# Low parts of the early weights made by VectorE alone, and a new table of priorities, in a one-core transformer block

## The chip, the cores and the metric

The kernel runs on one core of one Trainium2 chip. A core has TensorE (PE in the rows: matmuls and transposes), VectorE (DVE), ScalarE (ACT), GpSimd (POOL) and SyncE (SP, which here only issues DMAs). Each engine takes its own instructions strictly in order and waits on semaphores for the others. The metric is device microseconds (us) of one execution, the median of several runs; lower is better.

## The reference

One transformer block on 512 tokens of width 1024, all in 32-bit floats. Of the reference, this is what is computed:

```python
u = rmsnorm(h, norm_mix_g) @ w_in
c_q, c_kv, k_rope, q_nsa, kv_cmp, kv_slc, kv_win, gate_logits = split(u)
o_mla = mla_mixer(c_q, c_kv, k_rope, ...)     # 8 heads over latent q and kv
o_nsa = nsa_mixer(q_nsa, kv_cmp, kv_slc, kv_win, gate_logits, ...)
#   = g0 * attention over 31 compressed blocks + g1 * over selected keys + g2 * over a window
mixed = concat(rmsnorm(o_mla), rmsnorm(o_nsa))
h = h + mixed @ w_out
f = rmsnorm(h, norm_ffn_g)
h = h + (silu(f @ w_gate) * (f @ w_up)) @ w_down
return rmsnorm(h, final_norm_g)
```

With 512 tokens every block is selected and the window covers every earlier token, so the kernel computes both sparse branches as causal attention with a bias.

## The kernel before, in words

Every factor of a matmul is kept as a high part (the value rounded to the type `fp32r`) and a low part (value minus high part), and a product is three matmuls: high by high, high by low, low by high (lines 168 to 170, `mm3`). So each weight is loaded as it is (`w_raw`, 128 partitions by 1024 values, 512 KB), then copied to the high part by ScalarE or VectorE (line 392, `w_hi`), and the low part `w_lo` is the difference of the two, made by VectorE (line 394) or GpSimd (line 395). Each weight is split in two pieces of 128x512. Both inputs and the output of a low part lie in SBUF.

The stages follow each other with overlap. (1) The tokens are normed and transposed (`xTh`, `xTl`), and the latent columns of `w_in` (`wl_raw`, split in eight pieces of 128x440) are multiplied for each of four token tiles, normed (`cn`) and turned. (2) Eight projections of 24 matmuls of 128x512 each: four of queries (`qs`), two of keys (`kh`, `kl`), two that feed the compression (`rr`); two compression products over weights of 512 KB twice (`in_nsa_cmp_w...`), and the values. (3) Sparse and latent softmax attention: scores (`sc`), minimum on VectorE (line 829), exponential on ScalarE (834), scaling on GpSimd (840), transposes (845), high part on ScalarE (850), low part on VectorE (853), value products (879). The latent weights `ukr` and `uqr` and the output weights `w_out` are split in the same way while this goes on. (4) The output product, and a feed-forward part that makes its own weight pieces elsewhere (line 1396). The change doesn't touch that code.

The rings: `w_raw` has two buffers in stages 1 and 2, the split pairs have three, and a product accumulates in one of two PSUM banks named `mm`. A bank comes free when VectorE has read it for the low part of its result (`qs`, line 371).

What sets the order: a planner in the kernel (`Plan`, lines 52 to 116) knows every job with an estimate of its time and lays the instructions of all engines out when the program is built. Where a job may run on either of two engines, it compares when each could start, plus an offset for that engine (`pdve`, `ppool`, `pact`). Between jobs that could start, the lower priority number goes first. All these numbers stand in the table `PRI` (line 123). The chip then runs the order as it was laid out. The DMA queues in the traffic around stage 2: SyncE issues the loads of `w_raw`, then the bias tables `bn` (8 DMAs) and `ga` (8 DMAs), in its own order; ScalarE issues the first halves of 24 background sums `T` of `w_down` and GpSimd the second halves (lines 1356 and 1357). The DMAs of the two hardware queues share eight completion counters (DMAHW0 to DMAHW7) in turn, and a DMA waits until the one before it on its counter has landed.

Of the kernel before, what the change touches and what calls it, by code (L numbers as in the profile page):

```python
# [13 lines left out]
OP = mybir.AluOpType  # L14
# [19 lines left out]
def f(ap):  # L34
    return ap.bitcast(F32)
# [19 lines left out]
class Plan:  # L55
# [11 lines left out]
    def add(self, ways, fn=None, after=(), pri=0.0, takes=(), frees=(), lag=None):  # L67

        if fn is not None:
            ways = [(ways[0], ways[1] * (1.07 if ways[0] == "pe" and ways[1] < 1374 else 1.0), fn)]  # L70
        j = Job(ways, [a for a in after if a is not None], pri, takes, frees, lag)
        self.jobs.append(j)
        return j
# [13 lines left out]
    def run(self):  # L87
        busy = {}
        clock, ready, waiting = {"dma": 3500.0, "dma2": 3000.0}, [], list(self.jobs)
        while waiting or ready:  # L90
# [4 lines left out]
            for j in ready:  # L95
                if any(len(self.slots[s]) < j.takes.count(s) for s in j.takes):
                    continue
                for way in j.ways:
                    e = way[0]
                    issue = 1150 if e in ("dma", "dma2") else 0  # L100
                    t = max([clock.get(e, 0.0)] + [a.seen(e) + issue for a in j.after] + [min(self.slots[s]) + issue for s in j.takes])
                    best.setdefault(e, []).append((t + (PRI.get("p" + str(e), 0) if len(j.ways) > 1 else 0), j.pri, j, way, t))
            assert best, "no job can go on"
            picks = []
            for e, c in best.items():
                t0 = min(x[0] for x in c)
                picks.append(min((x for x in c if x[0] <= t0 + PRI["slack"]), key=lambda x: x[1]))
            _, _, j, way, t = min(picks, key=lambda x: (x[0], x[1]))
# [11 lines left out]

PRI = dict(k0=-5.4, q0=-12.1, v=51.3, ck=-13.0, k1=8.0, cv=-9.5, q1=-9.4, q2=-38.5, q3=12.6, mla=38.1, out=180.9, slack=0, pdve=20.1,
           ppool=72.3, pact=310.9, wload=-10.3, wsplit=-28.4, mkeys=-2.4, lat=-20.5, cmp=-18.4, cuse=94.3, use=17.0, sout=77.2, seven=183.9,
           xoff=-26.6, xstep=-35.5, bias=-61.8, sums=912.1, bout=-82.5, loff=-25.8, woff=-217.5, wstep=301.5)


@with_exitstack
def block_kernel(ctx: ExitStack, tc: tile.TileContext, I, out):
    nc = tc.nc  # L130
    ve, se, pe, gp, sy = nc.vector, nc.scalar, nc.tensor, nc.gpsimd, nc.sync
# [140 lines left out]
    add = plan.add  # L272
    late = {}

    def t_act(n, sb=False):
        return (95 if sb else 55) + 0.833 * n
# [4 lines left out]
    def t_dve(n):  # L281
        return 70 + 1.042 * n

    def t_copy(n):
        return 70 + 0.521 * n
# [4 lines left out]
    def t_pool(n):  # L290
        return 90 + 2.22 * n
# [9 lines left out]
    def load(dst, src, pri, after=()):  # L301
        n = int(np.prod(dst.shape)) * 4
        return add(("dma", max(n / 360.0, 480)), lambda: sy.dma_start(dst, src), after, pri, lag=950)
# [86 lines left out]
    def split_pieces(h, l, raw, n, after, pri, takes=(), frees=()):  # L390

        j = add([("act", t_act(n, True), lambda: se.copy(h(), raw())), ("dve", t_copy(n), lambda: ve.tensor_copy(h(), raw()))],  # L392
                None, after, pri, takes=takes)
        return add([("dve", t_dve(n), lambda: ve.tensor_tensor(l(), raw(), f(h()), op=OP.subtract)),
                    ("pool", t_pool(n), lambda: gp.tensor_tensor(l(), raw(), f(h()), op=OP.subtract))], None, [j], pri, frees=frees)  # L395

    def weight(pl, srcs, shape, pri, raw, part, nraw, npart, after=(), pieces=2, parts=None):

        w = {}
        n = int(np.prod(shape))  # L400

        def start():
            w["raw"] = pl().tile([P] + list(shape), F32, name="w_raw", tag="w_raw", bufs=nraw)
            for dst, src in srcs:
                sy.dma_start(dst(w["raw"]), src)

        def piece(c):
            return slice(c * shape[0] // pieces, (c + 1) * shape[0] // pieces)

        def room():  # L410
            w["h"], w["l"] = parts() if parts else [pl().tile([P] + list(shape), F32R, name=nm, tag=nm, bufs=npart) for nm in ("w_hi", "w_lo")]

        j = w["load"] = add(("dma", n * P * 4 / 360.0), start, after, pri + PRI["wload"], takes=[raw], lag=950)
        j = w["room"] = add((None, 0), room, [j], pri + PRI["wsplit"], takes=[part])
        return w, [split_pieces(lambda c=c: w["h"][:, piece(c)], lambda c=c: w["l"][:, piece(c)], lambda c=c: w["raw"][:, piece(c)], n // pieces,
                                [j], pri + PRI["wsplit"] + 0.1 * c, frees=[raw] if c == pieces - 1 else ()) for c in range(pieces)]

# [13 lines left out]
    def load_wl(u):  # L431
        sy.dma_start(wl_raw[:, u, :, 0:416], win[:, 2 * u:2 * u + 2, 0:416])
        sy.dma_start(wl_raw[:, u, :, 416:440], win[:, 2 * u:2 * u + 2, C_GATE:C_END])

    wl_ready = []
    for u in range(4):
        j = add(("dma", 1300), lambda u=u: load_wl(u), pri=-97 + (u if u < 3 else 4), lag=950)
        wl_ready += [split_pieces(lambda u=u, k=k: wl_parts[u][0][:, k], lambda u=u, k=k: wl_parts[u][1][:, k], lambda u=u, k=k: wl_raw[:, u, k],
                                  440, [j], -95 + PRI["woff"] + PRI["wstep"] * u) for k in range(2)]
    x_loaded = [x0] + [[load(xt[t], xv[:, t, :], (-94, -92, -91)[t - 1])] * 2 for t in range(1, NT)]  # L440
# [88 lines left out]
    def bias_rows(c0, c1):  # L529
# [20 lines left out]
        return add(("act", 80), out, [j] + wl_ready, PRI["bout"], frees=["s"], lag=6000)  # L550

    table = split_pieces(lambda: txp[:, 0], lambda: txp[:, 1], lambda: tx, H, [g_row], PRI["bias"])
    choice_used = []
    bias0 = [bias_rows(0, 320), bias_rows(320, 640)]
# [527 lines left out]
    for t in range(NT):  # L1082
# [3 lines left out]
        def go(d=d, ts=ts):  # L1086
            d["o"] = bank("mm")
            mm3(d["o"], kvTh[:, ts], kvTl[:, ts], flat(late["uvh"]), flat(late["uvl"]), True, True)

        j = add(("pe", 640), go, uv_ready + lat_done, mpri + t, takes=["mm"])  # L1090
        vm_ready += split_values(lambda t=t: late["vm"][:, t], lambda d=d: d["o"].rearrange("p (h d) -> p h d", h=H), S, [j], mpri + t)
    for q in range(2):
        qc = slice(384 * q, 384 * q + 384)
        for t in range(NT):
            pri = mpri + 4 + 4 * q + t
# [16 lines left out]
            j = add(("pe", 480), lambda go=go: go(0), [uq_ready[q][0]] + lat_done, pri, takes=["mm"])  # L1112
            j = add(("pe", 480), lambda go=go: go(1), [j, uq_ready[q][1]], pri)
            j = add(("act", t_act(256)), lambda qd=qd, ov=ov: se.copy(qd()[:, :, 0:64], ov()[:, :, 0:64]), [j], pri)
            j = add(("dve", 480), rope, [j], pri, frees=["mm"])
# [192 lines left out]
    for nh in range(2):  # L1308
        for t in range(NT):
# [7 lines left out]
            j = None  # L1317
            for k in range(4):
                j = add(("pe", 640), lambda k=k, go=go: go(k), [j, wo[2 * nh + k // 2][1][k % 2]] + sparse_jobs, opri + 4 * nh + t, takes=["mm"] if k == 0 else (),
                        frees=["part2"] if t == NT - 1 and k % 2 else ())  # L1320
# [4 lines left out]
    for nh in range(2):  # L1325
        for t in range(NT):
# [7 lines left out]
            j = None  # L1334
            for k in range(4):
                j = add(("pe", 640), lambda k=k, go=go: go(k), [j, wo[4 + 2 * nh + k // 2][1][k % 2]] + latent_jobs, 300 + 4 * nh + t,
                        takes=["mm"] if k == 0 else (), frees=["part2"] if t == NT - 1 and k % 2 else ())
# [603 lines left out]
```

## Time and profile before

| | |
|---|---|
| median of 3 runs | 644.17 us (644.1 to 644.45) |
| the profiled execution, its own time | 642.98 us |
| its span in the trace | 641.1 us |
| TensorE busy | 609.1 us, 95% |
| VectorE busy | 520.9 us, 81% |
| ScalarE busy | 369.6 us, 58% |
| GpSimd busy | 177.0 us, 28% |

Shares of the whole span are means over stages with different limits. In the feed-forward part TensorE has no gap; in the 300 us before it, gaps and a busy VectorE alternate.

### The profile page before, as it was taken

How to read it: one execution, taken by the hardware profiler on the slowest of the kernel's cores; microseconds unless marked ns; L12 is line 12 of the kernel's file. 1: busy time of each engine (PE TensorE's matmuls, PEld its weight loads, DVE VectorE, ACT ScalarE, POOL GpSimd, SP SyncE). 2: the span in 40 equal slices, each digit the busy share in tenths (PEclk: the TensorE clock that was granted, in tenths of full speed). 3: DMA queues.
4: the chain of work that ended last, by engine and by line, in shares of the span. 5: the costliest groups of instructions: out<-in, count | busy, mean ns of one | idle time of the engine just before them, and what ended most of it. 6: DMA issues, size and time to landing. Idle time of an engine off the chain costs nothing.

```text
span 641.1 us, 11228 instructions
## 1 busy us (share of the span) xinstructions
PE 609.1 (95%) x3973; PEld 540.8 (84%) x3973; DVE 520.9 (81%) x1078; ACT 369.6 (58%) x767; POOL 177.0 (28%) x252
## 2 busy tenths in 40 slices
PE   4999889999999989999999999999999999999994
PEld 2878677988887767887999999999999998888883
DVE  5856788589999898659978777887778999978846
ACT  3532248589898876334754455454455586458434
POOL 3632356357965683325000000000000000000003
PEclk9999899999999999999999999999999999999997
DMA  9635762463331863475584666655544366456503
GB/s 280 124 88 149 171 159 64 87 161 71 63 71 34 265 166 63 132 228 166 148 215 128 185 181 186 168 121 151 163 151 130 88 196 198 146 181 194 183 1 131
DMA packets 76297, 92.75 MB, mean 145 GB/s; under 512 B 10240, under 2 KB 49584, under 8 KB 76242
## 3 DMA queue, kind: packets, MB, share of 16 engines
q1 hardware_dynamic: 63248, 67.53, 34.2%
q0 software_dynamic: 6080, 11.75, 11.5%
q10 hardware_dynamic: 6914, 12.75, 6.9%
q8 instruction: 31, 0.51, 0.3%
q14 instruction: 24, 0.20, 0.1%
HBM read 89.24 MB, written 25.85 MB: 180 GB/s over the span
## 4 chain that ended last, share of the span: by engine, by line
PE 71%; DVE 13%; issue 5%; ACT 4%; DMA 3%; POOL 2%; SPq 0%; POOLq 0%; ACTq 0%; DVEq 0%
PE mm L168 9%; PE mm L170 9%; PE mm L169 9%; PE sc L170 7%; PE sc L169 7%; PE sc L168 7%; PE pv L169 3%; PE pv L170 3%; PE pv L168 3%; PE tp L845 3%; DMA w_raw<-in_w_in_dram 2%; PE pv L879 2%; DVE s L829 2%; DVE ptl L853 2%; PE tp L168 1%
## 5 line engine op out<-in xcount | busy, mean ns | idle before, releaser
L170 PE MATMUL sc<-fh,w_unit 128*128 128x256 f32 x352 | 98.5, 280 | 0.0
L168 PE MATMUL sc<-fh,w_unit 128*128 128x256 f32 x352 | 98.5, 280 | 0.0
L169 PE MATMUL sc<-fl,w_unit 128*128 128x256 f32 x352 | 98.2, 279 | 0.0
L1396 DVE TENSOR_TENSOR w_unit<-b_raw,w_unit 128x1024 fp32r<-128x1024 f32 (+1 forms) x54 | 63.9, 1183 | 25.5 <-ACT w_unit L1580 15.2
L169 PEld LDWEIGHTS sc<-fl,w_unit 128*128 128x128 f32 x352 | 66.2, 188 | 0.0
L170 PEld LDWEIGHTS sc<-fh,w_unit 128*128 128x128 f32 x352 | 66.1, 188 | 0.0
L168 PEld LDWEIGHTS sc<-fh,w_unit 128*128 128x128 f32 x352 | 65.8, 187 | 0.0
L834 ACT ACTIVATE s<-s,m 128x128 f32<-128x128 f32 (+3 forms) x96 | 53.6, 559 | 11.7 <-DVE m L829 11.2
L1396 DVE TENSOR_TENSOR w_unit<-b_first,w_unit 128x1024 fp32r<-128x1024 f32 (+1 forms) x34 | 40.0, 1175 | 24.4 <-ACT w_unit L1580 18.1
L840 POOL TENSOR_SCALAR s<-s,l,gates 128x128 f32<-128x128 f32 (+3 forms) x64 | 41.7, 667 | 30.2 <-DVE l L837 21.3
L170 PE MATMUL mm<-fh,w_unit 128*128 128x256 f32 x176 | 49.3, 280 | 0.0
L168 PE MATMUL mm<-fh,w_unit 128*128 128x256 f32 x176 | 49.1, 279 | 0.0
L169 PE MATMUL mm<-fl,w_unit 128*128 128x256 f32 x176 | 49.1, 279 | 0.0
L853 DVE TENSOR_TENSOR ptl<-tp,pth 128x128 fp32r<-128x128 f32 (+3 forms) x96 | 44.3, 482 | 3.6 <-ACT pth L850 2.9
L395 POOL TENSOR_TENSOR w_lo<-w_raw,w_hi 128x512 fp32r<-128x512 f32 x27 | 36.1, 1344 | 39.6 <-DVE w_hi L392 17.6
L850 ACT ACTIVATE pth<-tp 128x128 fp32r<-128x128 f32 (+3 forms) x96 | 39.0, 431 | 7.9 <-PE tp L845 4.7
L845 PE MATMUL tp<-ident,s 128*128 128x128 f32 x240 | 40.5, 277 | 2.2 <-DVE ptl L853 1.6
L1357 POOL DMA_DIRECT2D T<-T x12 | 13.1, 1095 | 99.1 <-DMA T<-in_w_down_dram 98.7
L1580 ACT CAST w_unit<-b_raw 128x1024 fp32r<-128x1024 f32 x32 | 33.6, 1051 | 11.4 <-PE pv L169 5.9
L1856 POOL TENSOR_SCALAR ss<-ss 128x1 f32<-128x1 f32 x9 | 3.2, 357 | 133.6 <-ACT xo L1853 133.5
L1357 POOL DMA_DIRECT2D T<-in_w_down_dram x12 | 13.4, 1117 | 85.9 <-DMA T<-in_w_down_dram 85.9
L845 PEld LDWEIGHTS tp<-ident,s 128*128 128x128 f32 x240 | 27.4, 140 | 9.7 <-POOL s L840 3.5
(366 smaller groups left out, 1976.6 us busy)
## 6 DMA issues: line engine op xcount, KB each, us to landing
T<-in_w_down_dram ACTq DMA_DIRECT2D x20, 512.0 KB, 4.1
b_first<-in_w_gate_dram SPq DMA_DIRECT2D x12, 512.0 KB, 4.4
b_raw<-in_w_up_dram SPq DMA_DIRECT2D x12, 512.0 KB, 6.5
T<-in_w_down_dram POOLq DMA_DIRECT2D x10, 512.0 KB, 6.8
T<-T POOLq DMA_DIRECT2D x10, 512.0 KB, 5.9
b_raw<-in_w_gate_dram SPq DMA_DIRECT2D x10, 512.0 KB, 4.2
b_late<-in_w_up_dram SPq DMA_DIRECT2D x10, 512.0 KB, 4.8
b_raw<-in_w_down_dram SPq DMA_DIRECT2D x10, 512.0 KB, 3.5
```

The source lines that it names most:

```text
L168: pe.matmul(o, lh, rh, start=start, stop=False, **kw)
L169: pe.matmul(o, lh, rl, start=False, stop=False, **kw)
L170: pe.matmul(o, ll, rh, start=False, stop=stop, **kw)
L395: ("pool", t_pool(n), lambda: gp.tensor_tensor(l(), raw(), f(h()), op=OP.subtract))], None, [j], pri, frees=frees)
L834: se.activation(c["s"][:, 0:n], c["s"][:, 0:n], AF.Exp, bias=c["m"], scale=-1.0, accum_out=c["l"])
L840: eng.tensor_scalar(c["s"][:, 0:n], c["s"][:, 0:n], c["l"], gate(), op0=OP.mult, op1=OP.mult)
L845: pe.transpose(c["tp"][:, j * P:(j + 1) * P], c["s"][:, j * P:(j + 1) * P], ident)
L850: se.activation(c["dh"], c["src"], AF.Copy)
L853: ve.tensor_tensor(c["dl"], c["src"], f(c["dh"]), op=OP.subtract)
L1357: j = wsum_done[name, u] = add(("pool", 1000), lambda o=o, name=name, second=second: gp.dma_start(o(name), second(), accum_op=OP.add, max_ ...
L1396: return add(("dve", t_dve(n)), lambda: ve.tensor_tensor(dst(), a(), b(), op=op), after, pri, **kw)
L1580: j = add(("act", t_act(n, True)), lambda: se.copy(w["p"][0], b()), [rw] + need, pri + 5)
```

## The change

Two edits. In `split_pieces` the way over GpSimd is removed, so that every low part of a weight outside the feed-forward part is made by VectorE. The function is called for the latent columns, for all `w_raw` weights, for the latent weights `ukr` and `uqr`, and for a few small tables. And the table `PRI` has new values throughout.

```diff
-PRI = dict(k0=-5.4, q0=-12.1, v=51.3, ck=-13.0, k1=8.0, cv=-9.5, q1=-9.4, q2=-38.5, q3=12.6, mla=38.1, out=180.9, slack=0, pdve=20.1,
+PRI = dict(k0=-2.63, q0=-9.94, v=42.62, ck=-11.94, k1=7.78, cv=-4.7, q1=-11.57, q2=-11.64, q3=-42.8, mla=45.5, out=279.1, slack=0, pdve=46.95,
...
-        return add([("dve", t_dve(n), lambda: ve.tensor_tensor(l(), raw(), f(h()), op=OP.subtract)),
-                    ("pool", t_pool(n), lambda: gp.tensor_tensor(l(), raw(), f(h()), op=OP.subtract))], None, [j], pri, frees=frees)
+        return add(("dve", t_dve(n)), lambda: ve.tensor_tensor(l(), raw(), f(h()), op=OP.subtract), [j], pri, frees=frees)
```

What this does to the order shows first on VectorE, at the splits of the fourth and fifth `w_raw` weights, between the projections. In the kernel before:

```order
L392 CAST w_hi<-w_raw 128x512 [waits DMAHW7_49,PE_49]
L392 CAST w_hi<-w_raw 128x512
L394 TENSOR_TENSOR w_lo<-w_raw,w_hi 128x512 [waits DVE_49,PE_49]
L371 SCALAR_TENSOR_TENSOR qs<-mm,qs 64x512 [waits Activation_49]
L371 SCALAR_TENSOR_TENSOR qs<-mm,qs 64x512
L392 CAST w_hi<-w_raw 128x512 [waits DMAHW0_49,PE_49]
```

The same place on VectorE in the changed kernel:

```order
L392 CAST w_hi<-w_raw 128x512 [waits DMAHW7_49,PE_49]
L392 CAST w_hi<-w_raw 128x512
L394 TENSOR_TENSOR w_lo<-w_raw,w_hi 128x512 [waits DVE_49,PE_49]
L371 SCALAR_TENSOR_TENSOR qs<-mm,qs 64x512 [waits Activation_49]
L394 TENSOR_TENSOR w_lo<-w_raw,w_hi 128x512 [waits DVE_49]
L371 SCALAR_TENSOR_TENSOR qs<-mm,qs 64x512
L392 CAST w_hi<-w_raw 128x512 [waits DMAHW0_49,PE_49]
```

The second low part, which GpSimd made before, now stands between the two `qs` that free the bank.

On SyncE's queue the weight loads and the bias tables change places. Before (the DMA `T_0_130`, which ScalarE issues, comes in turn on DMAHW1 here, between two of the `bn`):

```order
L595 DMA bn<-ldr 32x2x512 [waits DMAHW2_49]
L595 DMA bn<-ldr 32x2x512 [waits DMAHW3_49]
L405 DMA w_raw<-in_w_in_dram 128x8x128 [waits DMAHW4_49,DVE_49,Pool_49]
L603 DMA ga<-gdr 16x8x56 [waits DMAHW5_49,DMAHW1_49]
L603 DMA ga<-gdr 16x8x56 [waits DMAHW6_49]
L603 DMA ga<-gdr 16x8x56 [waits DMAHW7_49]
L603 DMA ga<-gdr 16x8x56 [waits DMAHW0_49]
L603 DMA ga<-gdr 16x8x56 [waits DMAHW1_49]
L603 DMA ga<-gdr 16x8x56 [waits DMAHW2_49]
L603 DMA ga<-gdr 16x8x56 [waits DMAHW3_49]
L603 DMA ga<-gdr 16x8x56 [waits DMAHW4_49]
L405 DMA w_raw<-in_w_in_dram 128x8x128 [waits DMAHW5_49,DVE_49,Pool_49]
```

In the changed kernel, where `T_0_130` comes in turn on DMAHW2:

```order
L594 DMA bn<-ldr 32x2x512 [waits DMAHW3_49]
L602 DMA ga<-gdr 16x8x56 [waits DMAHW4_49,DMAHW2_49]
L602 DMA ga<-gdr 16x8x56 [waits DMAHW5_49]
L602 DMA ga<-gdr 16x8x56 [waits DMAHW6_49]
L602 DMA ga<-gdr 16x8x56 [waits DMAHW7_49]
L602 DMA ga<-gdr 16x8x56 [waits DMAHW0_49]
L602 DMA ga<-gdr 16x8x56 [waits DMAHW1_49]
L602 DMA ga<-gdr 16x8x56 [waits DMAHW2_49]
L602 DMA ga<-gdr 16x8x56 [waits DMAHW3_49]
L404 DMA w_raw<-in_nsa_cmp_w_k_dram 128x8x128 [waits DMAHW4_49,DVE_49]
L404 DMA w_raw<-in_w_in_dram 128x8x128 [waits DMAHW5_49,DVE_49]
```

Behind `bn` and `ga` stood the weight of the fifth projection; now the second half of the first compression weight stands there, and the weight of the fourth projection, which stood between `bn` and `ga`, has moved ahead of both. On TensorE 96 projection matmuls stand before the first compression product instead of 72. Further counts from the order: VectorE makes 44 low parts of 128x512 instead of 17, all eight of 128x440 instead of four, and all eight of the latent weights instead of two; GpSimd makes 38 fewer. ScalarE takes two more of the squares at the start, GpSimd four more of the subtractions at the compressed softmax. The feed-forward part keeps its order.

## Rows read from the trace of the kernel before

**Rows 1.** Windows: stretch, busy us (instructions) of PE, PEld, DVE, ACT, POOL, granted clock, DMA.
```profile
14.20:19.50 5.30, 5.30 (x17) 4.75 (x16) 5.01 (x11) 3.16 (x9) 3.43 (x7) 1.00 1.00 234
19.50:44.00 24.50, 22.70 (x124) 18.89 (x123) 18.20 (x54) 10.68 (x35) 9.91 (x12) 1.00 0.52 105
65.20:67.86 2.66, 0.24 (x3) 0.16 (x3) 1.23 (x3) 0.83 (x2) 0.62 (x1) 0.95 0.90 260
67.86:70.98 3.12, 3.12 (x7) 2.45 (x8) 2.95 (x10) 0.38 (x2) 0.65 (x1) 0.50 0.16 48
80.00:105.00 25.00, 22.08 (x133) 18.93 (x132) 20.13 (x61) 14.70 (x41) 14.05 (x23) 1.00 0.55 131
140.00:200.00 60.00, 58.48 (x398) 51.07 (x396) 58.72 (x233) 54.93 (x168) 45.74 (x76) 1.00 0.33 73
200.00:262.00 62.00, 58.56 (x352) 46.22 (x353) 55.91 (x172) 48.73 (x131) 37.97 (x49) 1.00 0.51 143
302.00:622.00 320.00, 319.26 (x2303) 300.06 (x2302) 265.16 (x323) 173.76 (x226) 13.32 (x13) 1.00 0.55 157
```

**Rows 2.** What TensorE waited for, whole span: us in total, times, longest.
```profile
PE mm L168 <- DVE qs L371: 2.4, 1, 2.4
PE tp L349 <- DVE xTl L369: 2.1, 2, 1.5
PE tp L504 <- DVE cn L497: 1.2, 2, 0.9
PE mm L168 <- DVE vc L369: 1.1, 1, 1.1
PE sc L925 <- DVE qs L371: 1.0, 1, 1.0
```

**Rows 3.** Groups by line and form, GpSimd, whole span: count, busy us, mean ns, idle before.
```profile
L395 POOL TENSOR_TENSOR w_lo<-w_raw,w_hi 128x512 fp32r<-128x512 f32 x27 | 36.1, 1344 | 39.6 <-DVE w_hi L392 17.6 <-ACT w_hi L392 17.3 <-PE mm L170 4.1
L395 POOL TENSOR_TENSOR uql<-uqr,uqh 128x384 fp32r<-128x384 f32 x4 | 4.4, 1106 | 1.1 <-ACT uqh L392 1.1
```

**Rows 4.** Groups by line and form, VectorE, first 302 us.
```profile
L394 DVE TENSOR_TENSOR w_lo<-w_raw,w_hi 128x512 fp32r<-128x512 f32 x17 | 20.1, 1183 | 1.0 <-ACT w_hi L392 0.3
L392 DVE CAST w_hi<-w_raw 128x512 fp32r<-128x512 f32 x26 | 11.8, 485 | 9.5 <-PE mm L169 5.9 <-DMA w_raw<-in_w_in_dram 2.9 <-PE mm L170 0.6
```

**Rows 5.** Timeline of all engines, 50 to 68 us: start, duration, instruction, idle before and releaser.
```profile
50.23 0.39 PE L168 MATMUL mm<-xTh,w_hi 128*128 128x512 f32 x1
51.44 1.36 POOL L395 TENSOR_TENSOR w_lo<-w_raw,w_hi 128x512 fp32r<-128x512 f32 x1 [3.51 <-DVE w_hi L392]
51.74 1.60 DVE L394 TENSOR_TENSOR w_lo<-w_raw,w_hi 128x512 fp32r<-128x512 f32 x1
53.38 1.39 DVE L371 SCALAR_TENSOR_TENSOR qs<-mm,qs 64x512 fp32r<-64x512 f32 x2
56.55 0.69 ACTq L1356 DMA_DIRECT2D T<-in_w_down_dram  x1
...
61.56 0.39 PE L170 MATMUL mm<-xTh,w_lo 128*128 128x512 f32 x1
62.67 0.39 SPq L405 DMA_DIRECT2D w_raw<-in_w_in_dram  x1
66.56 0.43 DVE L392 CAST w_hi<-w_raw 128x512 fp32r<-128x512 f32 x1 [1.61 <-DMA w_raw<-in_w_in_dram]
67.86 0.77 PE L168 MATMUL mm<-xTh,w_hi 128*128 128x512 f32 x1 [2.42 <-DVE qs L371]
```

**Rows 6.** Timeline of VectorE, 30 to 33 us, where GpSimd is idle.
```profile
30.73 0.68 DVE L394 TENSOR_TENSOR w_lo<-w_raw,w_hi 128x512 fp32r<-128x512 f32 x1
```

**Rows 7.** Timeline of all engines, 83.5 to 86 us.
```profile
83.64 1.27 POOL L395 TENSOR_TENSOR w_lo<-w_raw,w_hi 128x512 fp32r<-128x512 f32 x1 [0.64 <-ACT w_hi L392]
84.29 0.90 DVE L392 CAST w_hi<-w_raw 128x512 fp32r<-128x512 f32 x1
```

**Rows 8.** What SyncE's queue waited for, first 300 us: us in total, times, longest.
```profile
SPq L603 <- DMA T<-in_w_down_dram: 5.0, 1, 5.0
```

**Rows 9.** The tile w_raw, whole span: time from issue to landing of its DMAs.
```profile
DMA to landing us min/median/max: 2.9/4.3/7.5
```

More of the change, by code (lines that the diff above doesn't have):

```diff
@@ L119, in run @@
         self.jobs = []
-PRI = dict(k0=-5.4, q0=-12.1, v=51.3, ck=-13.0, k1=8.0, cv=-9.5, q1=-9.4, q2=-38.5, q3=12.6, mla=38.1, out=180.9, slack=0, pdve=20.1,
-           ppool=72.3, pact=310.9, wload=-10.3, wsplit=-28.4, mkeys=-2.4, lat=-20.5, cmp=-18.4, cuse=94.3, use=17.0, sout=77.2, seven=183.9,
-           xoff=-26.6, xstep=-35.5, bias=-61.8, sums=912.1, bout=-82.5, loff=-25.8, woff=-217.5, wstep=301.5)
+PRI = dict(k0=-2.63, q0=-9.94, v=42.62, ck=-11.94, k1=7.78, cv=-4.7, q1=-11.57, q2=-11.64, q3=-42.8, mla=45.5, out=279.1, slack=0, pdve=46.95,
+           ppool=52.5, pact=411.27, wload=-37.81, wsplit=23.04, mkeys=11.16, lat=-0.05, cmp=-18.4, cuse=214.73, use=19.56, sout=88.09, seven=201.45,
+           xoff=-186.78, xstep=-23.66, bias=-62.89, sums=865.37, bout=-223.21, loff=-51.08, woff=-219.86, wstep=563.69)
 @with_exitstack
```

## The prediction, made before the result was known

> **What bounds the kernel now.** I read the windows by stage first [rows 1]. From 302 to 622 us TensorE is busy 319.26 of 320 us: the feed-forward part is full, its order stays, and nothing can be won or lost there except by when it starts. So the question is the first 302 us. There TensorE has gaps in two kinds of place. Between 19.5 and 44 us it idles 24.5 - 22.7 = 1.8 us, and between 80 and 105 us 2.9 us; between 140 and 262 us it idles only 1.5 + 3.4 us, but VectorE is busy 58.72 of 60 and 55.91 of 62 us. And one hole costs twice: it idles 65.2 to 67.86 us, and then runs 3.12 us at a granted clock of 0.50, which is 1.2 instead of 2.4 GHz, so it loses half of that, 1.5 us, once more. Next I read what TensorE waited for [rows 2]: VectorE every time, 2.4 us in that hole for `qs`, 2.1 for `xTl`, 1.2 for `cn`, 1.1 for `vc`, 1.0 for another `qs`. Last the timelines, for why VectorE was late.
>
> In the hole [rows 5] VectorE's cast of the fifth projection's weight, started at 66.56 us, had waited for its load, which SyncE issued only at 62.67 us. The second `qs` of the third projection stood behind that cast, and with it the bank that the fourth needs. The load was late because it stands behind `ga` in SyncE's queue, and one `ga` shares a completion counter with the background DMA `T`: the queue waited 5.0 us for it [rows 8], and `T` was issued at 56.55 us.
>
> **What the first edit is worth by itself.** Alone, VectorE makes a low part of 128x512 in 0.68 us [rows 6]. GpSimd needs 1.34 us on average for 27 of them, and 1.11 us for four of 128x384 [rows 3]. While GpSimd works on one, VectorE's own takes 1.60 us: it starts at 51.74, GpSimd ends at 51.44 + 1.36 = 52.80, VectorE 0.54 us later [rows 5]. So it stands still until GpSimd is done. Over 17 of them VectorE's mean is 1183 ns [rows 4], so 17 x (1183 - 680) = 8.6 us of its time is waiting for GpSimd. A pair of pieces made on both engines is complete after 53.34 - 51.44 = 1.9 us; both on VectorE would take 2 x 0.68 = 1.4 us. Casts suffer too: one took 0.90 us beside a GpSimd low part [rows 7], against a mean of 485 ns [rows 4].
>
> The bill for VectorE: 38 low parts more at 0.68 us or less are at most 26 us; 8.6 us come back on its own low parts, 26 x (485 - 430) = 1.4 us on the casts, taking 0.43 us [rows 5] for one that is not held up. Some 16 us at most are added over 302 us, and only those in the busy stretch can hurt.
>
> The Trainium skill (SBUF — State Buffer, Who interferes with whom) says that VectorE instructions with two SBUF inputs and GpSimd instructions that read SBUF exclude each other for a whole instruction. The 1.60 us agree. It says too that an instruction with one SBUF input outside VectorE's two-port modes is not held up, so by that rule the softmax instructions that read PSUM gain nothing from the freed GpSimd; I find no row against it and count no gain for them.
>
> **Term by term.**
>
> Start and latent stage, to 44 us: four more low parts of 128x440 and four of 128x512 on VectorE's line, but two squares go to ScalarE and the pairs finish sooner. TensorE waits 2.1 us for `xTl` and 1.2 for `cn` here [rows 2]. I take -1.0 us. At best both waits go: -3.3. At worst a new wait: the first weight's low parts now stand among VectorE's other work, so its buffer comes free later, the third weight loads later, and the last two `cn` stand behind the cast that waits for it; the longest such wait in the rows is 1.61 us [rows 5], so +1.6.
>
> The hole at 65 us: this is where I expect the gain that does not come. The changed queue has the fourth projection's weight ahead of the bias tables. But the second half of the first compression weight stands behind them now, and the counter of `T` still sits before it, with two `ga` behind the wait instead of four; `T` again follows the second projection on ScalarE. On the clock of before: that load starts at most 1 us sooner, at 61.8, and lands after the same 3.9 us at 65.7. VectorE then has to go through two casts (2 x 0.43), two low parts (2 x 0.68) and two `qs` (1.39), 3.6 us, before the third projection's bank is free for the compression product: 69.3. TensorE has one projection more before that point. A projection is 24 matmuls, and 50 starts between 50.23 and 61.56 us [rows 5] give 0.227 us each, so 5.4 us: it arrives at 61.8 + 5.4 = 67.2 and waits 2.1 us. The compression product takes 65.2 - 61.8 = 3.4 us, to 72.7; the next cast, two low parts and two `qs` behind it again take 3.6 us, to 72.9: 0.2 us more. 2.3 us against 2.4: I take 0. At best the wait and its half clock go, -2.4 - 1.5 = -3.9. At worst the load lands after 7.5 us, the longest seen [rows 9], instead of 3.9: +3.6.
>
> 80 to 105 us: the wait of 1.0 us for `qs` is behind the cast of 0.90 us [rows 7], of which 0.47 was waiting for GpSimd; the 1.1 us for `vc` come behind further held-up low parts. More projections stand ahead of the sparse softmax. I take -1.5 us, half the idle time; at best all 2.9 go, at worst one wait of the size of the longest there is added, +1.1.
>
> 140 to 262 us: 12 low parts come to VectorE (six of `w_out`, six of the latent weights), at most 12 x 0.68 = 8.2 us, on an engine with 122 - 114.6 = 7.4 us free. GpSimd gives up 12, some 8.1 us for six and 4.4 us for four of the latent ones [rows 3], so the scaling of the softmax waits less behind them. TensorE has filling matmuls (latent, then output products) while VectorE works. I take 0; at best -2 (two fifths of TensorE's idle 4.9), at worst +4 (half of what is added).
>
> The new priorities elsewhere I cannot price, and cover by the range. Sum: -1.0 + 0 - 1.5 + 0 = -2.5 us. The profiled execution took 642.98 us (span 641.1 and 1.9 around it), so it would take 640.5; the median of the runs is 1.2 above the profiled one, so 641.7.
>
> **The rivals.** A, the holes close: the load lands early, or VectorE gets past it, and TensorE keeps its full clock: -3.9 and the -1.0, -1.5 and half of -2 give 7.4 us, 636.8. For it: VectorE waits for GpSimd at most projections; against: the counter.
>
> B, nothing to see: the earlier low parts only move waits, because VectorE passes the same instructions in order and the `T` counter sets the same times: 644.2. For it: every TensorE wait named is for VectorE's results, not low parts; against: the held-up cast [rows 7].
>
> C, slower by the load: the second half of the compression weight lands after 7.5 us. TensorE stands still 3.6 us longer, which takes the gains with it: 644.2 - 2.5 + 3.6 = 645.3, and 647.8 if the other gains stay out too. I price it at 647. It decides from a landing later than 3.9 + 2.5 = 6.4 us after its issue.
>
> D, VectorE becomes the bound from 140 to 262 us: +4 there gives 641.7 + 4 = 645.7. For it: 97.9% busy in 140 to 200 [rows 1]; against: it gives back waiting time and some subtractions and squares to GpSimd. The Trainium skill (Perfetto Trace Analysis, Optimizing Scalar/DVE Operations) has the rule that speaks for D: with VectorE saturated, work may be moved to GpSimd. The same sentence warns that the two share a read port, so that it may not help; rows 5 show that warning, rows 1 the saturation.
>
> **How the numbers follow.** The forecast's own case 0.36 (own range 639 to 642.8), A 0.20, B 0.18, C 0.16, D 0.10. A measurement of this kernel can tell about 0.2%, 1.3 us: faster is the forecast and A, 0.56; same is B, 0.18; slower is C and D, 0.26. The range 636 to 647.5 leaves out the far ends of A and C. Predicted: 641.7 us.
>
> **What would show it.** In the profile after: VectorE's `w_lo` at a mean near 0.7 us in 44 instances and no line of GpSimd for them; VectorE busy some 5 to 15 us more; a TensorE wait of about 2 us before the first compression product near 66 us instead of after it, with a stretch at half clock behind it; waits for `cn` and `xTl` smaller; idle in 80 to 105 us near 1.5. It is wrong if the half clock has gone (A), if that wait exceeds 4 us (C), or if TensorE idles over 7 us between 140 and 262 us (D).

## The result, and the profile after

The changed kernel takes 647.97 us (median of 4 runs, 646.92 to 648.3) against 644.17: a ratio of 1.0055, 95% interval 1.0038 to 1.0073. It is 3.8 us slower, where 641.7 us had been predicted. The profiled execution took 648.1 us, with a span of 646.3 against 641.1: 5.2 us more. Of the 83 further executions of the kernel before that were timed beside the experiments, only 10 had a mean granted clock as high as the profiled one's 0.992 (0.991 or more), with a median of 642.1 us against 644.7 for the other 73, so that part of the 5.2 us is the choice of the execution.

The edit itself did to the instructions what was expected. Groups of VectorE's instructions after the change (output and inputs, shape, count, then busy us, mean ns, and the idle time ahead of them with what ended it):

```profile
L394 DVE TENSOR_TENSOR w_lo<-w_raw,w_hi 128x512 fp32r<-128x512 f32 x44 | 30.1, 700 | 0.9 <-ACT w_hi L392 0.7
L392 DVE CAST w_hi<-w_raw 128x512 fp32r<-128x512 f32 x24 | 9.7, 434 | 17.7 <-DMA w_raw<-in_nsa_cmp_w_k_dram 7.1 <-DMA w_raw<-in_w_in_dram 5.2 <-PE mm L169 4.5
```

All 44 low parts are on VectorE at a mean of 700 ns, where 17 had a mean of 1183 and GpSimd's 27 one of 1344 [rows 3, 4], and the casts fell from 485 to 434 ns. VectorE is busy 523.8 us, only 2.9 more than before. But the second row's last columns show casts that stand and wait for loads, 12.3 us in all. What TensorE waited for (line, releaser, us in total, times, longest) shows what came of that:

```profile
PE mm L714 <- DVE qs L371: 3.8, 1, 3.8
PE mm L168 <- DVE cr_v L174: 3.5, 1, 3.5
...
PE tp L349 <- DVE xTl L369: 0.9, 1, 0.9
```

The wait for `xTl` fell from 2.1 to 0.9 us [rows 2], as hoped. The two waits at the top stand where before there was one of 2.4 us. The stretches by time (length, busy us of PE, PEld, DVE, ACT and POOL with counts, granted clock, DMA share, GB/s), the first of the new stall, the others those of [rows 1]:

```profile
38.00:44.00 6.00, 2.50 (x12) 1.30 (x11) 4.23 (x20) 2.45 (x12) 1.19 (x2) 1.00 0.36 100
...
80.00:105.00 25.00, 23.51 (x125) 19.18 (x124) 20.45 (x61) 8.31 (x24) 8.96 (x17) 0.97 0.55 135
140.00:200.00 60.00, 56.17 (x388) 49.68 (x387) 58.33 (x232) 52.78 (x163) 39.34 (x68) 1.00 0.38 85
200.00:262.00 62.00, 58.71 (x360) 45.71 (x359) 58.63 (x185) 51.87 (x140) 31.35 (x44) 1.00 0.50 137
```

And TensorE alone, behind the two long waits (length, busy us, clock, DMA share, GB/s):

```profile
67.90:71.70 3.80, 0.06 (x1) 0.95 0.54 149
71.70:81.00 9.30, 9.22 (x38) 0.50 0.41 113
81.00:82.00 1.00, 1.00 (x5) 0.72 0.00 0
...
44.40:47.00 2.60, 2.60 (x11) 0.50 0.00 0
47.00:48.00 1.00, 1.00 (x6) 0.79 0.00 0
```

The second stall costs 3.8 us of standing still, and then TensorE works for 9.3 us at a clock of 0.50, 1.2 GHz, and one more at 0.72: another 4.65 + 0.28 = 4.9 us. Before it was 2.42 + 1.5 = 3.9 us [rows 1], so 4.8 more. The first stall is made up for by the head start, since the first projection begins at 43.43 us (44.08 before), but its half clock costs 1.3 + 0.2 = 1.5 us. Part of that head start belongs to this execution. The first matmuls of 440 columns follow each other in 0.37 us, later ones in 0.20 (the clock of 1.00 in the first line of [rows 1] doesn't tell them apart); they get faster near 17 us here, but near 20 us in the profile of before and near 20 us in the run with all sums later below. That run has the same order up to here, and its first projection begins at 44.95 us. From 80 to 105 us the idle time is 1.5 us instead of 2.9. So -0.65 + 1.5 + 4.8 - 1.4 = 4.2 us; measured, the last three matmuls that read the tokens (`xTh`, `xTl`) start at 137.81 us instead of 134.10, 3.7 later; this point is called the end of the projections below. From there to the first feed-forward product it takes 168.94 instead of 167.44 us, 1.5 more; both give the 5.2. The feed-forward part has its old length.

Why VectorE was late at 39.9 us. The timeline after the change (start, us, engine, line, operation):

```profile
32.11 2.35 SPq L404 DMA_DIRECT2D w_raw<-in_w_in_dram  x2
...
38.77 0.76 DVE L392 CAST w_hi<-w_raw 128x512 fp32r<-128x512 f32 x2 [4.23 <-DMA w_raw<-in_w_in_dram]
...
40.65 0.18 DVE L485 TENSOR_TENSOR cn<-mm,rc 128x32 f32<-128x32 f32 x1
...
42.54 0.48 DVE L496 SCALAR_TENSOR_TENSOR cn<-mm,cr_r,gqkv 128x256 f32<-128x256 f32 x1 [0.87 <-POOL cr_r L176]
...
43.43 0.47 PE L168 MATMUL mm<-xTh,w_hi 128*128 128x512 f32 x1 [3.50 <-DVE cr_v L174]
```

VectorE's cast of the third projection's weight waits for its load, issued at 32.11 and there at 38.77 us, and the third latent tile, whose bank the first projection needs, stands behind it. Why it was late at 67.9 us:

```profile
51.41 10.69 SPq L602 DMA_DIRECT2D ga<-gdr  x8
...
61.62 1.30 POOL L1356 DMA_DIRECT2D T<-in_w_down_dram  x1 [14.47 <-DMA T<-in_w_down_dram]
62.20 0.39 SPq L404 DMA_DIRECT2D w_raw<-in_nsa_cmp_w_k_dram  x1
...
68.11 0.76 DVE L392 CAST w_hi<-w_raw 128x512 fp32r<-128x512 f32 x2 [7.07 <-DMA w_raw<-in_nsa_cmp_w_k_dram]
70.94 0.69 DVE L371 SCALAR_TENSOR_TENSOR qs<-mm,qs 64x512 fp32r<-64x512 f32 x1
71.78 0.45 PE L714 MATMUL mm<-rr,w_hi 128*128 128x136 f32 x1 [3.82 <-DVE qs L371]
```

The load behind `ga` is issued at 62.20 us, where 61.8 was predicted, TensorE arrives at 67.96 us (67.2), and from the cast to the end of the second `qs` it takes 3.5 us (3.6). But from its issue to the cast the load takes 5.9 us instead of 3.9. Just ahead of it GpSimd issues the second half of the sum `T`. From 65.5 to 68 us GpSimd's queue (q0) fills the DMA engines, and SyncE's (q1), with the load, moves next to nothing (packets, MB, share of the engines' time):

```profile
q0 software_dynamic: 224, 0.46, 100.3%
q1 hardware_dynamic: 168, 0.08, 14.6%
```

In the kernel before, GpSimd's queue reads:

```profile
71.04 1.30 POOL L395 TENSOR_TENSOR w_lo<-w_raw,w_hi 128x512 fp32r<-128x512 f32 x1 [2.53 <-DVE w_hi L392]
72.28 1.29 POOL L1357 DMA_DIRECT2D T<-in_w_down_dram  x1
```

There the same transfer stood behind this low part, of the next weight, and behind one at 67.24 us, of the weight whose load stood behind `ga` there; so it could not start until that load had landed. With the low parts gone from GpSimd it starts 10.7 us sooner, onto the load. The trace of before held the sign of it: the load that SyncE issued there at 73.09 us, just behind `T`, took 7.1 us. That was the theory to test.

### The profile page after: what moved, and what is told of

Read it like the earlier page. It is cut to its first block, busy times and chain, and to the rows that moved or that the text cites. A ratio compares the mean times of both kernels' runs of the same rounds, so it can differ in the third digit from the quotient of the medians.

```text
span 646.3 us, 11200 instructions
## 1 busy us (share of the span) xinstructions
PE 611.9 (95%) x3973; PEld 544.1 (84%) x3973; DVE 523.8 (81%) x1101; ACT 372.5 (58%) x775; POOL 139.7 (22%) x221
## 4 chain that ended last, share of the span: by engine, by line
PE 71%; DVE 13%; ACT 5%; issue 4%; DMA 3%; POOL 2%; SPq 0%; POOLq 0%; ACTq 0%; DVEq 0%
PE mm L168 9%; PE mm L170 9%; PE mm L169 9%; PE sc L168 7%; PE sc L170 7%; PE sc L169 7%; PE pv L168 3%; PE pv L170 3%; PE pv L169 3%; PE pv L878 2%; PE tp L844 2%; DVE ptl L852 2%; DVE s L828 2%; ACT s L833 2%; DMA w_raw<-in_w_in_dram 2%
## 5 line engine op out<-in xcount | busy, mean ns | idle before, releaser
L1713 ACT CAST w_unit<-b_raw 128x1024 fp32r<-128x1024 f32 (+1 forms) x22 | 21.4, 974 | 23.8 <-PE mm L170 8.2
L170 PEld LDWEIGHTS mm<-fh,w_unit 128*128 128x128 f32 x176 | 33.1, 188 | 0.0
```

The lines of the kernel that those rows point to most:

```text
L170: pe.matmul(o, ll, rh, start=False, stop=stop, **kw)
L1713: j = add(("act", t_act(512 * n, True)), lambda: se.copy(w["p"][0], raw()), [rw, ld], pri + 1)
```

## The experiments

GpSimd had 37 low parts before the change (the count from the order and the prediction say 38). In all runs the planner's order, of the kernel before or of the changed one, was written out as a list and laid as it is, so that only what is named differs; "before" in each comparison is the kernel before on the same chip. First, each order with the other engine.

**Low parts back on GpSimd, in the changed order.**

```diff
-  37 low parts: ve.tensor_tensor(...)
+  37 low parts: gp.tensor_tensor(...)     # each at its place in the changed order
```

> The changed kernel's order of work on every engine is kept, instruction for instruction; only the 37 low parts that GpSimd made before the change go back to GpSimd, each at its place in the order. Theory O (the new order costs the time, the edit itself does not): no better than the change, 648 to 652 us, because the two long stalls of TensorE (3.5 us at 39.9 us and 3.8 us at 67.9 us) stay and GpSimd's low parts take 1.34 us instead of 0.68. Theory V (37 low parts more on VectorE cost the time): 643 to 645.5 us, as before the change, and the idle time of TensorE from 140 to 262 us falls from 7.1 to about 5 us.

Measured: 653.46 us, 1.0146 (1.0122 to 1.0169), above both ranges. Theory V falls: with the edit undone the time rises by 5.5 us. The timeline around the second stall:

```profile
62.16 0.39 SPq L405 DMA_DIRECT2D w_raw<-in_nsa_cmp_w_k_dram  x1
...
66.38 0.76 DVE L392 CAST w_hi<-w_raw 128x512 fp32r<-128x512 f32 x2 [5.25 <-DMA w_raw<-in_nsa_cmp_w_k_dram]
...
68.27 1.29 POOL L1357 DMA_DIRECT2D T<-in_w_down_dram  x1
```

The same load, issued at the same time, takes 4.2 us, and `T` is issued after it. TensorE waits only 1.7 us, yet again some 10 us at a clock of 0.50 follow. Most of the 5.5 us arises later: the projections end at 138.50 us (137.81 in the changed kernel), and from there to the first feed-forward product it takes 172.5 us instead of 168.9.

**Low parts on VectorE, in the order of before.** The same exchange the other way round:

```diff
-  37 low parts: gp.tensor_tensor(...)
+  37 low parts: ve.tensor_tensor(...)     # each at its place in the order of before
```

> The order of the kernel before is kept on every engine; only the 37 low parts of GpSimd go to VectorE, each at its place in the order. Theory O: 641.5 to 644.5 us, the edit alone is worth 0 to 2.5 us. Theory V: 646.5 to 649 us, with TensorE idle over 7 us from 140 to 262 us.

Measured: 651.54 us, 1.0129 (1.01 to 1.0159), above both ranges. Theory O falls too: the edit alone, in the old order, costs 7.4 us. Theory V's sign doesn't come either: TensorE idles 2.56 + 3.88 = 6.4 us from 140 to 262 us. The timeline:

```profile
62.46 1.30 POOL L1356 DMA_DIRECT2D T<-in_w_down_dram  x1 [13.06 <-DMA T<-in_w_down_dram]
...
64.00 0.39 SPq L404 DMA_DIRECT2D w_raw<-in_w_in_dram  x1
...
70.59 0.43 DVE L392 CAST w_hi<-w_raw 128x512 fp32r<-128x512 f32 x1 [4.68 <-DMA w_raw<-in_w_in_dram]
...
71.89 0.76 PE L168 MATMUL mm<-xTh,w_hi 128*128 128x512 f32 x1 [4.99 <-DVE qs L371]
```

Here `T` is issued 10 us sooner than before, and the load of [rows 5] takes 6.6 us instead of 3.9; TensorE waits 5.0 us for it. Neither the edit nor the order is the cause by itself, but what both leave to GpSimd.

**The cast behind the third latent tile**, on VectorE in the changed order:

```diff
-L392 CAST w_hi<-w_raw 128x512 x2
-L394 TENSOR_TENSOR w_lo<-w_raw,w_hi 128x512 x2
 L485 TENSOR_TENSOR cn<-mm,rc 128x32
...
 L497 SCALAR_TENSOR_TENSOR cn<-mm,cr_r,gqkv 128x128
+L392 CAST w_hi<-w_raw 128x512 x2
+L394 TENSOR_TENSOR w_lo<-w_raw,w_hi 128x512 x2
```

> The changed kernel with one move on VectorE: the two casts and two low parts of the third projection's weight stand behind the scaling of the third latent tile instead of ahead of its rotation. Theory O: the wait of 3.5 us at 39.9 us goes, and with it the half clock from 44.4 to 47.6 us (some 1.6 us); all that follows comes earlier, the second stall with it: 5.1 us less, 642.5 to 644 us. If the second stall has its end set by its load alone, it grows by what is won and the time stays at 647 to 648. Theory V: 646 to 648 us, since VectorE's amount of work stays.

Measured: 647.78 us, 1.0055 (1.0036 to 1.0074): nothing. The wait is down to 1.5 us. But the next stall stands where it stood:

```profile
43.45 0.55 PE L168 MATMUL mm<-xTh,w_hi 128*128 128x512 f32 x1 [1.50 <-DVE cn L497]
...
62.24 0.39 SPq L404 DMA_DIRECT2D w_raw<-in_nsa_cmp_w_k_dram  x1
...
71.86 0.45 PE L714 MATMUL mm<-rr,w_hi 128*128 128x136 f32 x1 [3.87 <-DVE qs L371]
```

This profile alone doesn't decide it, since its latent tiles began 2 us later; the median does. A later run repeats the move with the second stall gone.

**The load ahead of `ga`**, in SyncE's queue:

```diff
 L594 DMA bn<-ldr 32x2x512 x8
+L404 DMA w_raw<-in_nsa_cmp_w_k_dram 128x8x128
 L602 DMA ga<-gdr 16x8x56 x8
-L404 DMA w_raw<-in_nsa_cmp_w_k_dram 128x8x128
```

> The changed kernel with one move in SyncE's queue: the load of the second half of the first compression weight stands ahead of the eight loads of the table ga, no longer behind them. Theory O: this load is issued near 59.7 us, when its buffer is free, instead of 62.2 us, and lands ahead of the background transfer's second part; TensorE's wait of 3.8 us at 67.9 us shrinks to under 1.5 us, and the half clock of 9.6 us behind it shortens or goes: 642.5 to 646.5 us. Theory V: 647 to 648.5 us.

Measured: 645.87 us, 1.0022 (1.0005 to 1.0038), 2.1 us less than the change. The load is issued even sooner than expected, and TensorE waits one weight later instead:

```profile
56.08 0.39 SPq L404 DMA_DIRECT2D w_raw<-in_nsa_cmp_w_k_dram  x1
...
75.10 0.76 PE L168 MATMUL mm<-xTh,w_hi 128*128 128x512 f32 x1 [1.91 <-DVE qs L371]
```

**Only GpSimd's half of the sums held back**, in GpSimd's queue (the later sums move with it):

```diff
-L1356 DMA T_0_130<-in_w_down_dram 128x2x512
 L939 TENSOR_TENSOR s<-s,m 128x4x32 x2
 L950 TENSOR_TENSOR l<-l,gates 128x4
 L951 TENSOR_TENSOR s<-s,l 128x4x32
+L1356 DMA T_0_130<-in_w_down_dram 128x2x512
```

> The changed kernel; only GpSimd's background transfers for the sums T (and the ScalarE halves after the first) are issued later: the first one stands behind the first instructions of the sparse softmax in GpSimd's queue, near 92 us, and no longer at 61.6 us. Theory C (with no low parts in its queue GpSimd issues this transfer 10 us sooner than before the change, and it slows the weight's load that is issued at 62.2 us): the load lands in about 4 us instead of 5.9, TensorE's wait before the first compression product falls from 3.8 to about 1.9 us, and the time to 645 to 646.5 us. Rival (the load is slow for another reason): wait and time stay, 647.3 to 648.6 us.

Measured: 646.42 us, 1.0026 (1.0011 to 1.0041), 1.5 us less than the change:

```profile
63.55 0.39 SPq L404 DMA_DIRECT2D w_raw<-in_nsa_cmp_w_k_dram  x1
...
67.93 0.76 DVE L392 CAST w_hi<-w_raw 128x512 fp32r<-128x512 f32 x2 [5.33 <-DMA w_raw<-in_nsa_cmp_w_k_dram]
...
71.60 0.30 PE L714 MATMUL mm<-rr,w_hi 128*128 128x136 f32 x1 [2.09 <-DVE qs L371]
```

The load takes 4.4 us, and the wait is 2.1: so the collision is shown, in both directions. Half clock still follows, over 6.9 us instead of some 10.

**All sums later**, ScalarE's halves too (some 35 us), in the changed kernel:

```diff
-  first sum: ScalarE 57.1 us, GpSimd 61.6 us
+  first sum: ScalarE 93.8 us, GpSimd 98.1 us
```

> The changed kernel with all background transfers for the sums T issued later, the first by some 35 us, both its halves. Theory C with the counter: neither ga nor the load behind it waits for T; the load is issued before 60 us and lands before TensorE arrives near 67.6 us; the wait of 3.8 us and the 9.6 us at half clock go, 640.5 to 643.5 us. Rival (VectorE's chain of casts, low parts and qs holds TensorE one weight later, as when ga was moved): 645 to 646.5 us.

Measured: 641.57 us, 0.9937 (0.991 to 0.9964): 6.4 us less than the change, and faster than the kernel before. SyncE's queue (start, us, line, transfers):

```profile
53.38 3.74 SPq L602 DMA_DIRECT2D ga<-gdr  x8
57.22 0.39 SPq L404 DMA_DIRECT2D w_raw<-in_nsa_cmp_w_k_dram  x1
```

And TensorE over the place of the second stall (length, busy us, clock, DMA share, GB/s):

```profile
65.20:75.00 9.80, 9.75 (x61) 1.00 0.26 71
75.00:80.00 5.00, 5.00 (x25) 1.00 0.61 182
```

`ga` takes 3.7 us instead of 10.7, the load is issued 5 us sooner, and in this profile TensorE neither waits nor loses its clock. The load itself takes 5.2 us here with no `T` near it (4.3 to 5.9 in the four other runs of the changed order with the sums later), and why is not shown; but it starts so early that nothing waits for it. The stall is the work of `T` twice over: its first half holds SyncE's queue by the counter, its second slows the load.

**The same in the kernel before.**

```diff
-  first sum: ScalarE 56.6 us, GpSimd 72.3 us
+  first sum: ScalarE 99.8 us, GpSimd 108.7 us
```

> The kernel before with all background transfers for the sums T issued later by some 35 us. Theory C with the counter: the fifth projection's weight is loaded near 58 us instead of 62.7; the wait of 2.4 us at 65.4 us and the half clock behind it (1.5 us) go: 640 to 642 us. Rival: the wait only moves to the next weight, 643.5 to 644.5 us.

Measured: 644.53 us, 0.9995 (0.9976 to 1.0014), no gain: the rival was right. The weight is loaded 3.3 us sooner (59.42 us) and the wait falls from 2.4 to 1.3 us, but the half clock behind it stays (a mean of 0.83 from 65.2 to 75 us in both), and a new one comes at 84 us. TensorE's stretch there with the sums later (length, busy us, clock, DMA share, GB/s):

```profile
84.00:92.00 8.00, 6.99 (x25) 0.57 0.49 132
```

And the same stretch in the kernel before:

```profile
84.00:92.00 8.00, 6.78 (x38) 1.00 0.58 162
```

TensorE idles no more in this stretch than before, but now at half clock, 6.99 x 0.43 = 3.0 us. Why the clock falls in the one and not in the other the rows don't tell, nor whether the later sums have a part in it; this stays open.

**Order of before, VectorE alone, sums later.** Against the run before this one:

```diff
-  37 low parts: gp.tensor_tensor(...)
+  37 low parts: ve.tensor_tensor(...)
```

> The order of the kernel before, all low parts on VectorE (the run that took 651.5 us), and all background transfers for the sums T issued later. Theory C: its load of 6.6 us and its wait of 5.0 us go, with the half clock behind it; the edit alone is then worth what it is worth elsewhere: 642.5 to 646 us. Rival (37 low parts more on VectorE cost the time in themselves): 648 to 651 us.

Measured: 646.52 us, 1.0034 (1.0019 to 1.0048), 0.5 above theory C's range: 5.0 of the 7.4 us go. The wait of 5.0 us is down to 0.33. What is left, 2.0 us against the run before it, is the edit in an order that was laid for GpSimd.

**Changed order, GpSimd, sums later**, the last corner of this square. Against the changed kernel with the sums later:

```diff
-  37 low parts: ve.tensor_tensor(...)
+  37 low parts: gp.tensor_tensor(...)
```

> The changed kernel's order with the 37 low parts back on GpSimd, and all sums T later: the counterpart, in engine alone, of the run that took 641.6 us. If the edit by itself is worth something in this order once the sums are out of the way: 644 to 648 us. If all that the edit did was to let GpSimd issue the sums' transfer sooner: 641 to 642.5 us, the same as with VectorE.

Measured: 643.78 us, 0.999 (0.9975 to 1.0006). The first guess misses by 0.2 us, the second by more. The eight medians together:

| order | low parts | sums as they were | sums later |
|---|---|---|---|
| before | GpSimd and VectorE | 644.2 | 644.5 |
| before | VectorE | 651.5 | 646.5 |
| changed | GpSimd and VectorE | 653.5 | 643.8 |
| changed | VectorE | 648.0 | 641.6 |

With the sums later, VectorE alone is worth 2.2 us in the changed order and costs 2.0 in the old one. Most of both arises behind the projections: from their end to the first feed-forward product the traces show 169.9 us with VectorE against 171.8 with GpSimd in the changed order, and 169.9 against 168.3 in the old one. With the sums early, three of four are bad, and the kernel before is the one that gets past them.

**Sums later, and the cast behind the third latent tile.** Both edits above together; on VectorE, as above:

```diff
-  cast and low parts of the third weight, then the third latent tile
+  the third latent tile, then cast and low parts of the third weight
```

> The run with all sums T later (641.6 us), and in addition the two casts and two low parts of the third projection's weight behind the scaling of the third latent tile. Theory O: with the second stall gone, what is won at 39.9 us is no longer lost behind the load: the wait there falls from 3.0 to 1.5 us, 639 to 640.5 us; the half clock from 44 to 48 us may stay. Rival (the move is worth nothing, as before): 641 to 642.5 us.

Measured: 639.28 us, 0.9922 (0.9899 to 0.9944), the lowest median of the study, 2.3 us below the run without the move. But that run was made on another chip, and its interval (0.991 to 0.9964) overlaps this one: that the move is worth more once the stall behind it is gone is suggested, not shown.

**Sums later, the late stage as before.** From the end of the projections the list goes on in the order of the kernel before, with its 15 low parts on GpSimd:

```diff
-  jobs planned behind 130 us: changed order, low parts on VectorE
+  jobs planned behind 130 us: order of before, 15 low parts on GpSimd
```

> The run with all sums T later; from the end of the projections near 130 us on, all engines follow the order of the kernel before, and the 15 low parts that GpSimd made there go back to it; ahead of that nothing is changed. Theory D (the late stage, 140 to 262 us, is worse in the changed order with VectorE making the low parts there): TensorE's idle time in 140 to 262 us falls from 7.3 to about 5 us and the time to 639 to 640.5 us. Rival (what stands there follows from how the early stage ends): 641 to 642.5 us.

Measured: 641.14 us, 0.9935 (0.9911 to 0.9959), the same as without. TensorE in the late stage:

```profile
140.00:200.00 60.00, 57.10 (x384) 1.00 0.30 64
200.00:262.00 62.00, 58.64 (x351) 1.00 0.49 138
```

The idle time falls from 7.3 to 6.3 us, not to 5, and from the last projection to the first feed-forward product it takes 169.8 us (169.9 without). Theory D isn't borne out: with both put back, the order there and GpSimd's low parts, the 1.5 us stay. The same profile shows that half clock can come without a wait. Up to the end of the projections its order is that of the run without; TensorE idles 0.05 us from 68 to 71.5 us, through the 32 short matmuls of the compression product, and then its clock falls, where it stayed at 1.00 in the profile above:

```profile
68.00:71.50 3.50, 3.45 (x31) 1.00 0.04 10
71.50:74.90 3.40, 3.40 (x9) 0.50 0.51 154
```

**Seven idle matmuls in the first wait**, on top of the run with the cast moved:

```diff
 L534 MATMUL tp<-choice,txp 8x504 x4
+L1880 MATMUL pv<-xTh 128x512 x7
 L168 MATMUL mm<-xTh,w_hi 128x512
```

> The run with the sums later and the casts moved, and seven idle matmuls of 128x512 into a bank that nobody reads, ahead of the first projection, where TensorE waits 1.5 us: it is priced here what the half clock behind that wait costs. If the clock falls because TensorE stands still: full clock from 44 to 48 us, 1.5 us less than without the seven, 637.5 to 639 us. If not: the same time or up to 0.3 us more.

Measured: 639.42 us, 0.9925 (0.9904 to 0.9947), no gain. TensorE from 44 to 48 us without the seven (length, busy us, clock, DMA share, GB/s):

```profile
44.00:46.00 2.00, 2.00 (x8) 0.65 0.05 8
46.00:48.00 2.00, 1.95 (x7) 0.50 0.37 106
```

And with them:

```profile
44.00:46.00 2.00, 1.03 (x7) 1.00 0.54 163
46.00:48.00 2.00, 2.00 (x11) 1.00 0.88 250
```

The clock stays full in this profile, but TensorE reaches the turning of the fourth tile sooner and waits for it:

```profile
40.09 1.89 PE L1880 MATMUL pv<-xTh 128*128 128x512 f32 x7
...
44.97 0.52 PE L503 MATMUL tp<-ident,cn 128*128 128x128 f32 x3 [1.15 <-DVE cn L496]
```

That the seven kept the clock up isn't shown: one profile stands against one, and the mean clocks of six executions each overlap (0.992 to 0.997 without the seven, 0.994 to 0.997 with them).

## Why the prediction was wrong

**The step that failed** is the hole at 65 us, "on the clock of before: that load starts at most 1 us sooner, at 61.8, and lands after the same 3.9 us". The queue, the counter and the place of the wait were right, and TensorE's arrival nearly so. Two sizes were not. The landing took 5.9 us, because the edit took the low parts out of GpSimd's queue, behind which the second half of `T` had waited; the prediction followed `T` on ScalarE and never looked for its other half. It shows when the load alone is compared: 5.9 and 6.6 us where `T`'s second half is issued 0.6 and 1.5 us ahead of it, 3.9, 4.2 and 4.4 us where it starts later. The length alone would not prove it, with 4.3 to 5.9 us in this order without any `T` near; the traffic of the two queues and the run with GpSimd's half held back do. The range had allowed for up to 7.5 us, but as an accident and not as a consequence of the change. And the half clock was taken over at its old size, 1.5 us. Behind the wait there now stood the compression product, and TensorE ran through all of it, and six matmuls of the projection after it, at 1.2 GHz: 4.9 us. Together the term came to 4.8 us, where 0 was taken and +3.6 was the worst end.

**Start and latent stage** (-1.0 taken, +1.6 at worst): the mechanism of the bad end came true word for word, the third load late and the tiles behind the cast that waits for it. Its size was 3.5 us of waiting where the longest VectorE wait of the rows, 1.6 us, had been taken, and 1.5 us of half clock had not been counted at all. The gain at the start came too (`xTl` 2.1 to 0.9 us), so that in this profile the stage lost about 0.9 us (1.5 - 0.65), with a start that other executions of the same order didn't have. What the first stall costs in the end is not settled, since the gain from moving the cast isn't clear of the noise.

**80 to 105 us** (-1.5): right, 2.9 to 1.5 us of idle time. With the sums later, the changed order has 2.3 us there with GpSimd's low parts and 1.2 with VectorE's, so the freed VectorE has a part in it, and so, it seems, has the order.

**140 to 262 us** (0): TensorE idles 3.83 + 3.29 = 7.1 us instead of 4.9, just over the bound that was set for rival D, and the stretch from the last projection on is 1.5 us longer. But D's reason, VectorE as the bound, isn't supported: with GpSimd's low parts back in the changed order it idles 8.2 us (3.54 + 4.64), and with the old order and GpSimd's low parts back behind the sums' later start nothing is gained. Only in the order of before does VectorE alone lengthen this stretch, by 2.1 us (169.55 instead of 167.44). What makes the 1.5 us stays open.

**VectorE's bill** was right in its parts (700 and 434 ns) and too high in the sum: 2.9 us more, where 5 to 15 were expected.

**Rival C** was nearest, with 647 us, and it named the load; but it put the point from which it decides at a landing of 6.4 us, and 5.9 did, because it too left the half clock out; its sign, a wait over 4 us, was just missed at 3.8.

The page rule weighed in the prediction (the Trainium skill, SBUF — State Buffer, Who interferes with whom) agrees with the runs as far as they go: without GpSimd's low parts VectorE's own fell from 1183 to 700 ns. That the whole became slower is no argument against it; the lock was indeed gone.

## What to carry to other kernels

When work leaves an engine that takes its instructions in order, list what stood behind it in that queue, DMA issues above all: they now start sooner, and the profile before shows them at their old place only. A wait of TensorE is to be priced together with the half clock that may follow, and as a range: here some 10 us at half clock came behind waits of 3.8 and of 1.7 us, 6.9 behind one of 2.1, and 3.4 with hardly any wait. And an order that was laid for one distribution of the work is no test bed for another: here the same edit was worth anything from -5.5 to +7.4 us.

## What the runs showed of the hardware

Behind `ga`, a load of 512 KB took 5.9 and 6.6 us where GpSimd's transfer of 512 KB had been issued up to 1.5 us ahead of it, and 3.9 to 4.4 us in three runs where that came later; with no such transfer near it took 3.7 to 5.9 us in the seven runs with the sums later. In 2.5 us of the collision GpSimd's queue moved 0.46 MB and SyncE's 0.08. TensorE's clock stood at 0.50 for 9.3 us after a wait of 3.8 us, with 32 short matmuls of 136 and 68 columns first; for 3.1 us after 2.7 us of idling with matmuls of 512 columns behind it [rows 1]; and for 3.4 us behind the same 32 matmuls at full clock, with 0.05 us of idling among them. In the one profile with seven matmuls that nobody reads, over 1.9 us of a wait, it stayed at 1.00.
